# Keeping the partial sums of the seven-product pairs in two held PSUM banks

## The chip, the cores and the metric

The kernel runs on one core of one Trainium2 chip. The time is that of the device, in microseconds (us), from launch to end of one execution; the median of three runs of the kernel before is 1907.0 us (1905.99 to 1907.22).

## The reference

The reference is a trunk of two layers over 512 tokens of 1024 channels, in float32. Each layer has a feed-forward block, a token mixer (a convolution module in the first, stick-breaking attention in the second) and another feed-forward block. The change concerns the feed-forward blocks alone:

```
def swiglu_ffn(x, w_gate, w_up, w_down):
    return (jax.nn.silu(x @ w_gate) * (x @ w_up)) @ w_down
...
    h = h + HALF_STEP * swiglu_ffn(rms_norm(h, ffn1_norm[layer]), ...)
```

`w_gate` and `w_up` are 1024 x 2816 and `w_down` is 2816 x 1024, for each of the four blocks.

## The kernel before, in words

**Layout.** Channels lie on the 128 partitions, the 512 tokens along the free dimension, so the 1024 channels are eight tiles of 128 x 512, and the 2816 features of a block are 22 tiles, `f` = 0 to 21, worked in three thirds (`THIRDS`: 0 to 7, 8 to 15, 16 to 21). The four blocks are `ffn(0)` to `ffn(3)`. To keep float32 accuracy every operand is split into a rounded high part and a rest (`split`, L249 on ScalarE for the high part, L250 on VectorE for the rest), and every product is three matmuls: high by high, high by low, low by high.

**An ordinary pair.** For a feature tile, gate and up are two products of eight channel tiles and three matmuls each: 48 matmuls of 512 columns into two PSUM banks (L397 to L399). VectorE multiplies both banks by the norm's factor `rb` (L609, L611), ScalarE takes the Silu (L610), VectorE multiplies gate by up (L612), and the result is split into `hhi`, `hlo`. After a third, eight down products (`pd`) go to one bank each and are added to the residual stream by VectorE (L631).

**A seven-product pair.** In `ffn(1)` to `ffn(3)` the 32 tiles named in `SEVEN` (11, 10 and 11 of them) are made in another way, by the function `seven` (from L532): gate and up, the two halves of the channels and the two halves of the tokens form a 2 x 2 block product, which takes seven half-size products in place of eight:

```
SEVEN = {1: (5, 6, 8, 9, 11, 12, 14, 16, 17, 19, 20),
...
for q in range(NC // 2):
    PE.matmul(d, a[0], b[0], ...); PE.matmul(d, a[0], b[1], ...); PE.matmul(d, a[1], b[0], ...)
```

So a product is 12 matmuls of 256 columns (L555 to L557), and a pair 84. The products are named by their left operand: `11`, `12`, `22` (quarters of the weights) and `s1` to `s4` (sums of quarters, made on VectorE by `sevens`, L344 to L350). Their right operands are halves of `norm.x` (in the trace `xhi_f`, `xlo_f`) or sums `t` (`thi`, `tlo`). In the trace `11` and `12` are the matmuls with `xhi_f`/`xlo_f` and `whi`/`wlo`; `s1`, `s2` those with `sh`/`sl`; `s3`, `22` those with `thi`/`tlo` and `whi`/`wlo`; `s4` those with `uh`/`ul`.

The four results, gate (`tg`) and up (`tu`) for each half of the tokens, are these sums:

- gate, first half: `11` + `12`
- gate, second half: `11` + `s2` + `s1` + `s4`
- up, second half: `11` + `s2` + `s3` + `s1`
- up, first half: `11` + `s2` + `s3` + `22`

Before the change a pair takes three banks, `at_[0]` to `at_[2]`, of the seven of the pool `ps`. ScalarE copies `11` and `s1` to SBUF (`m1`, `m5`, L560 and L564); VectorE makes `v6` = `s2` + `m1` (L562) and `v7` = `s2` + `s3` + `m1` (L566), adds these to the banks (L568, L574, L575) and multiplies by `rb` (L571, L572, L576).

**Order.** Tiles, slots and semaphores come from the framework. The order in which each engine takes its instructions is fixed when the program is built: the text's order sets the priority, and an instruction whose operands would not be there is passed by later ones that can go. In the trace the matmuls of one pair stand among those of the next pair and of ordinary pairs. In the trace each engine then goes through its list in order: one that waits holds up those behind it. The next weights are fetched when a unit is taken (`unit`, `fetch`): DMA by the SyncE queue, then the split on ScalarE and VectorE, with three buffers of `raw`, `whi` and `wlo`, and for the second half of a seven-product pair's weights and for its sums one buffer each.

Of the kernel before, what the change touches and what calls it, by code (L numbers as in the profile page):

```python
# [6 lines left out]
F32 = mybir.dt.float32  # L7
# [7 lines left out]
P = 128  # L15
D = 1024
T = 512
# [181 lines left out]
def decoder_kernel(ctx, tc, xin, gu, dna, dnb, pw1, pw2, kq, wv, wo, out):  # L199
    nc = tc.nc  # L200
    V, A, G, PE = nc.vector, nc.scalar, nc.gpsimd, nc.tensor
# [35 lines left out]
    onesr = const.tile([P, P], F32R, name="onesr")  # L237
# [252 lines left out]
    def ffn(idx, norm, done, early=None, beside=None, sums=None, late=None, tail=None):  # L490
        with ExitStack() as c:
            hp = pool(c, f"hid{idx}")
            if beside is not None:
                pp_ = pool(c, f"beside{idx}")
            ps = pool(c, f"ps{idx}", space=PSUM)
            beside_hidden[0] = hp
            rb = norm.factor(ps) if idx else None
            halves = [slice(0, T // 2), slice(T // 2, T)]
            right = []

            def right_sums(q):


                x = []
                for k in (2 * q, 2 * q + 1):
                    f = tp.tile([P, T], F32, name=f"xs{idx}_{k}", tag="sq", bufs=2)
                    V.tensor_add(f, *(y.bitcast(F32) for y in norm.x[k]))
                    x.append(f)
                b11, b12, b21, b22 = (y[:, h] for y in x for h in halves)
                t = hp.tile([P, 2 * T], F32, name=f"ts{idx}_{q}", tag="st", bufs=STS)  # L510
                t1, t2, t3, t4 = (t[:, j * T // 2 : (j + 1) * T // 2] for j in range(4))
                V.tensor_sub(t1, b12, b11)
                V.tensor_sub(t2, b22, t1)
                V.tensor_sub(t3, b22, b12)
                V.tensor_sub(t4, b21, t2)
                tiles = [sums_at(q, o) for o in range(2)]
                for o, (h, l) in enumerate(tiles):
                    split(h, l, t[:, o * T : (o + 1) * T])
                right.append(tiles)
# [12 lines left out]
            def seven(n, tg, tu):  # L532
                w = unit()

                def x(row, h):
                    return lambda q: [y[:, halves[h]] for y in norm.x[2 * q + row]]

                def t(j):
                    return lambda q: [y[:, halves[j % 2]] for y in right[q][j // 2]]


                at_ = [
                    ps.tile([P, T], F32, name=f"pg{n}_{j}", tag="ps", bufs=7)[:, : T // 2]
                    for j in range(3)
                ]
                m1, m5, v6, v7 = (
                    hp.tile([P, T // 2], F32, name=f"{m}_{n}", tag=m, bufs=1)
                    for m in ("m1", "m5", "v6", "v7")
                )

                def product(j, left, rhs, first):
                    for q in range(NC // 2):
                        a, b, d = w[left](q), rhs(q), at_[j]
                        last_ = q == NC // 2 - 1
                        PE.matmul(d, a[0], b[0], start=first and q == 0, stop=False, skip_group_check=True)  # L555
                        PE.matmul(d, a[0], b[1], start=False, stop=False, skip_group_check=True)  # L556
                        PE.matmul(d, a[1], b[0], start=False, stop=last_, skip_group_check=True)  # L557

                product(0, "11", x(0, 0), True)
                A.copy(m1, at_[0])  # L560
                product(1, "s2", t(1), True)
                V.tensor_add(v6, at_[1], m1)  # L562
                product(2, "s1", t(0), True)
                A.copy(m5, at_[2])  # L564
                product(1, "s3", t(2), False)
                V.tensor_add(v7, at_[1], m1)  # L566
                product(2, "s4", x(1, 1), False)
                V.tensor_add(tg[:, halves[1]], at_[2], v6)  # L568
                product(0, "12", x(1, 0), False)
                product(1, "22", t(3), False)  # L570
                V.tensor_mul(tg[:, halves[1]], tg[:, halves[1]], rb[:, halves[1]])  # L571
                V.tensor_mul(tg[:, halves[0]], at_[0], rb[:, halves[0]])  # L572
                last[0] = A.activation(tg, tg, AF.Silu)
                V.tensor_add(tu[:, halves[1]], v7, m5)  # L574
                V.tensor_add(tu[:, halves[0]], at_[1], m1)  # L575
                V.tensor_mul(tu, tu, rb)  # L576

            for third, (f0, f1) in enumerate(THIRDS):
                hid = []
                for f in range(f0, f1):  # L580
                    n = f"{idx}_{f}"
                    if f in SEVEN.get(idx, ()):
                        tg = hp.tile([P, T], F32, name=f"tg{n}", tag="tg", bufs=2)
                        tu = hp.tile([P, T], F32, name=f"tu{n}", tag="tu", bufs=2)
                        seven(n, tg, tu)
                        V.tensor_mul(tu, tu, tg)  # L586
                        hi = hp.tile([P, T], F32R, name=f"hhi{n}", tag="hhi", bufs=8)
                        lo = hp.tile([P, T], F32R, name=f"hlo{n}", tag="hlo", bufs=8)
                        split(hi, lo, tu)
                        hid.append((hi, lo))  # L590
                        continue
                    pt = [ps.tile([P, T], F32, name=f"pg{n}_{o}", tag="ps", bufs=7) for o in range(2)]
                    if rb is None:
                        w = [unit() for o in range(2)]
                        for i, k in enumerate(norm.order):
                            for o in range(2):
                                mm3(pt[o], at(w[o], k * P, P), norm.x[k], i == 0, i == NC - 1)
                        with tc.issue_after(last[0].ins):
                            for k in range(NC):
                                norm.square(k)  # L600
                        rb = norm.factor(ps)
                    else:
                        for pp in pt:
                            w = unit()
                            for i, k in enumerate(norm.order):
                                mm3(pp, at(w, k * P, P), norm.x[k], i == 0, i == NC - 1)
                    tg = hp.tile([P, T], F32, name=f"tg{n}", tag="tg", bufs=2)
                    tu = hp.tile([P, T], F32, name=f"tu{n}", tag="tu", bufs=2)
                    V.tensor_mul(tg, pt[0], rb)  # L609
                    last[0] = A.activation(tg, tg, AF.Silu)  # L610
                    V.tensor_mul(tu, pt[1], rb)  # L611
                    V.tensor_mul(tu, tu, tg)  # L612
                    hi = hp.tile([P, T], F32R, name=f"hhi{n}", tag="hhi", bufs=8)
                    lo = hp.tile([P, T], F32R, name=f"hlo{n}", tag="hlo", bufs=8)
                    split(hi, lo, tu)
                    hid.append((hi, lo))
                    if f < NC // 2 and idx in SEVEN:
                        right_sums(f)
                    if early is not None and f == f0:
                        early(third, rb)  # L620
                    if beside is not None and (third or f > 1):
                        with tc.issue_after(last[0].ins):
                            beside(pp_)
                if third == 2 and late is not None:
                    late()
                for d in range(NC - TAIL if tail is not None and third == 2 else NC):
                    w = unit()
                    pd = ps.tile([P, T], F32, name=f"pd{idx}_{third}_{d}", tag="ps", bufs=7)
                    for j in range(f1 - f0):
                        mm3(pd, at(w, j * P, P), hid[j], j == 0, j == f1 - f0 - 1)  # L630
                    V.scalar_tensor_tensor(  # L631
                        res[d], pd, 0.5, res[d], op0=ALU.mult, op1=ALU.add
                    )
                    if third == 2:
                        done(d)
                    if beside is not None and d in (2, 5):
                        with tc.issue_after(last[0].ins):
                            beside(pp_)
# [5 lines left out]
    with ExitStack() as c:  # L644
        wm = pool(c, "wm")
        ps = pool(c, "pswm", space=PSUM)
# [7 lines left out]
    first = [opened() for o in range(2)]  # L654
# [51 lines left out]
    with ExitStack() as c:  # L706
        cv = pool(c, "cv")
        ps = pool(c, "pscv", space=PSUM)
        mshift = cv.tile([P, P], F32R, name="mshift")
        V.tensor_scalar_mul(mshift, ones, -1.0 / P)  # L710
        rb = tp.tile([P, T], F32, name="r_mix_0", tag="r", bufs=1)
# [327 lines left out]
        for d in SECOND[3:]:  # L1039
            w = None if d in HELD else unit()  # L1040
# [14 lines left out]
    with ExitStack() as c1:  # L1055
# [30 lines left out]
        with ExitStack() as c:  # L1086
            ap = pool(c, "at")
            ps = pool(c, "psat", space=PSUM)
# [391 lines left out]
```

## Time and profile before

| | |
|---|---|
| median of three runs | 1907.0 us |
| span of the profiled execution, first to last instruction | 1904.9 us |
| TensorE (PE) busy | 1884.1 us |
| VectorE (DVE) busy | 1318.5 us |
| ScalarE (ACT) busy | 872.7 us |
| matmuls | 10236 |

The profiled execution has no time of its own beside its span; the span is 2.1 us under the median of the runs. In the rows of the profile, times are in us unless marked ns; PE is the matmul, PEld the weight load that runs beside it. A row of the grouped lines gives line, engine, operation, output and inputs, shape, count, then busy time in us, mean ns of one, and after the second bar the engine's idle time just before them with what ended it. A row of the timeline gives start, duration, engine, line, operation and tiles. In the windows view a row has the stretch, its length, and the busy time and instruction count of each engine.

### The profile page before, as it was taken

What the parts mean: (1) busy time and instruction counts of PE and PEld (TensorE: products, weight loads), DVE (VectorE), ACT (ScalarE), POOL (GpSimd) and SP (SyncE); (2) the same over time, 40 slices, a digit from 0 to 9 for tenths busy, and PEclk for the clock granted to TensorE, in tenths of its full rate; (3) what the DMA queues carried; (4) which work ended last, traced back from release to release, by engine and by line L of the source; (5) the groups of instructions that cost most, each with busy time, mean ns of one, the idle gap of its engine ahead of it and who ended that gap; (6) DMA issues with size and microseconds to landing.
All of it is one profiled execution on the core that took longest, in us unless ns stands there. A gap on an engine that the chain in (4) does not pass through costs nothing.

```text
span 1904.9 us, 26577 instructions
## 1 busy us (share of the span) xinstructions
PE 1884.1 (99%) x10236; PEld 1630.4 (86%) x10236; DVE 1318.5 (69%) x2139; ACT 872.7 (46%) x1385; POOL 288.1 (15%) x267
## 2 busy tenths in 40 slices
PE   9999999999999999999999999999999999999997
PEld 7888888878998889898888988888888788898896
DVE  6544434589869577576775857778989688676575
ACT  5423424586644234244333423446778644343333
POOL 0212302079700000000000000004554100000001
PEclk9999999999999999999999999999999999999998
DMA  5756746444422323333433232442323133332322
GB/s 203 251 180 232 275 146 216 158 172 144 161 78 89 105 89 117 100 94 96 143 111 100 89 111 89 127 155 83 89 70 93 49 123 100 100 95 95 111 86 70
DMA packets 74254, 237.84 MB, mean 125 GB/s; under 512 B 8464, under 2 KB 11152, under 8 KB 74128
## 3 DMA queue, kind: packets, MB, share of 16 engines
q1 hardware_dynamic: 65776, 209.41, 34.0%
q10 hardware_dynamic: 8352, 26.74, 3.8%
q8 instruction: 80, 1.31, 0.3%
q14 instruction: 46, 0.38, 0.1%
HBM read 200.46 MB, written 31.46 MB: 122 GB/s over the span
## 4 chain that ended last, share of the span: by engine, by line
PE 94%; DVE 2%; POOL 1%; ACT 1%; issue 1%; DMA 0%; POOLq 0%; DVEq 0%; ACTq 0%
PE pg L397 11%; PE pg L398 11%; PE pg L399 11%; PE pd L398 8%; PE pd L397 8%; PE pd L399 8%; PE pg L557 6%; PE pg L556 6%; PE pg L555 6%; PE z L1192 2%; PE pa L397 1%; PE pa L398 1%; PE pa L399 1%; PE pv L397 1%; PE pk L397 1%
## 5 line engine op out<-in xcount | busy, mean ns | idle before, releaser
L249 ACT CAST whi<-raw 128x1024 fp32r<-128x1024 f32 (+2 forms) x310 | 313.2, 1013 | 634.6 <-PE pd L398 226.8
L250 DVE TENSOR_TENSOR wlo<-raw,whi 128x1024 fp32r<-128x1024 f32 (+2 forms) x310 | 367.8, 1191 | 43.1 <-ACT whi L249 42.7
L398 PE MATMUL pg<-xlo_f,whi 128*128 128x512 f32 x896 | 349.7, 391 | 0.0
L397 PE MATMUL pg<-xhi_f,whi 128*128 128x512 f32 x896 | 349.0, 391 | 0.6 <-ACT whi L249 0.6
L399 PE MATMUL pg<-xhi_f,wlo 128*128 128x512 f32 x896 | 349.4, 390 | 0.0
L398 PE MATMUL pd<-hlo,whi 128*128 128x512 f32 x686 | 266.2, 389 | 0.0
L399 PE MATMUL pd<-hhi,wlo 128*128 128x512 f32 x686 | 265.1, 389 | 0.0
L397 PE MATMUL pd<-hhi,whi 128*128 128x512 f32 x686 | 264.1, 389 | 0.0
L397 PEld LDWEIGHTS pg<-xhi_f,whi 128*128 128x128 f32 x896 | 169.0, 189 | 35.2 <-ACT whi L249 1.5
L399 PEld LDWEIGHTS pg<-xhi_f,wlo 128*128 128x128 f32 x896 | 168.6, 188 | 34.7 <-DVE wlo L250 0.3
L398 PEld LDWEIGHTS pg<-xlo_f,whi 128*128 128x128 f32 x896 | 168.8, 188 | 33.6
L631 DVE SCALAR_TENSOR_TENSOR xpar<-pd,xpar 128x512 f32<-128x512 f32 x93 | 63.7, 689 | 170.6 <-PE pd L399 170.6
L399 PEld LDWEIGHTS pd<-hhi,wlo 128*128 128x128 f32 x686 | 128.8, 188 | 26.8
L397 PEld LDWEIGHTS pd<-hhi,whi 128*128 128x128 f32 x686 | 128.8, 188 | 26.7
L398 PEld LDWEIGHTS pd<-hlo,whi 128*128 128x128 f32 x686 | 128.8, 188 | 26.6
L1092 POOL TENSOR_SCALAR_AFFINE_SELECT tri<-ones 128x128 f32<-128x128 f32 x1 | 0.6, 592 | 703.7 <-DVE tu L612 703.7
L250 POOL TENSOR_TENSOR plo<-praw,phi 128x1024 fp32r<-128x1024 f32 x24 | 59.0, 2461 | 275.7 <-ACT phi L249 273.9
L875 POOL TENSOR_TENSOR ws<-ws,pr 128x256 f32<-128x256 f32 (+1 forms) x90 | 91.0, 1023 | 58.2 <-ACT pr L873 54.6
L249 ACT CAST hhi<-tu 128x512 fp32r<-128x512 f32 x88 | 54.3, 621 | 87.9 <-DVE tu L586 49.2
L886 DVE SCALAR_TENSOR_TENSOR pc<-gl,xpar,pc 128x512 f32<-128x512 f32 (+1 forms) x145 | 88.3, 646 | 3.9 <-PE pc L865 2.2
L611 DVE TENSOR_TENSOR tu<-pg,r_f 128x512 f32<-128x512 f32 x56 | 38.6, 689 | 74.2 <-PE pg L399 74.2
L556 PE MATMUL pg<-tlo,whi 128*128 128x256 f32 x256 | 72.5, 283 | 0.0
(359 smaller groups left out, 4195.0 us busy)
## 6 DMA issues: line engine op xcount, KB each, us to landing
raw<-in_gu_dram SPq DMA_DIRECT2D x174, 512.0 KB, 3.5
raw<-in_dna_dram SPq DMA_DIRECT2D x64, 512.0 KB, 3.6
praw<-in_pw_dram SPq DMA_DIRECT2D x24, 512.0 KB, 4.4
aparth<-phi ACTq DMA_DIRECT2D x24, 512.0 KB, 2.7
apartl<-plo ACTq DMA_DIRECT2D x24, 512.0 KB, 3.8
raw<-in_dnb_dram SPq DMA_DIRECT2D x32, 384.0 KB, 3.4
whi<-aparth SPq DMA_DIRECT2D x21, 512.0 KB, 3.3
wlo<-apartl SPq DMA_DIRECT2D x21, 512.0 KB, 4.2
```

The lines of the kernel that those rows point to most:

```text
L249: ins = A.copy(dst_hi, src)
L250: (G if on_pool else V).tensor_sub(dst_lo, src, dst_hi.bitcast(F32))
L397: PE.matmul(ps, w[0], x[0], start=first, stop=False)
L398: PE.matmul(ps, w[0], x[1], start=False, stop=False)
L399: PE.matmul(ps, w[1], x[0], start=False, stop=last)
L555: PE.matmul(d, a[0], b[0], start=first and q == 0, stop=False, skip_group_check=True)
L556: PE.matmul(d, a[0], b[1], start=False, stop=False, skip_group_check=True)
L557: PE.matmul(d, a[1], b[0], start=False, stop=last_, skip_group_check=True)
L611: V.tensor_mul(tu, pt[1], rb)
L631: V.scalar_tensor_tensor(res[d], pd, 0.5, res[d], op0=ALU.mult, op1=ALU.add)
L875: add("G", 1.28 * f + 0.1 * half, lambda pr=pr: G.tensor_add(accp, accp, pr()[:, at0]), r=[pr], w=[at_], rank=rank)
L886: add("V", 0.66 * f + 0.06 * half, lambda x=x, q=q: V.scalar_tensor_tensor(pc(), x(), q, pc(), op0=ALU.mult, op1=ALU.add), r=[gl], w=[pc], ...
```

## The change

A pair takes two banks of its own, `g0` and `m`, and two banks `u0`, `g1` are held from the first feature tile of the block to the last seven-product pair, shared by all its pairs. ScalarE copies `11` from `g0` into `u0`, on which `s2` accumulates; it copies that sum from `u0` into `g1`, on which `s4` accumulates, while `s3` and then `22` accumulate on `u0`. `v6`, `v7` and `m1` go; `m5` gets two buffers. Two matmuls at the first feature tile of each of the three blocks write `u0` and `g1` once (`seed_banks`), so that later ones add to what stands there. The products, their number, and the tiles of `SEVEN` stay; the order of the products in the text changes from `11`, `s2`, `s1`, `s3`, `s4`, `12`, `22` to `11`, `s1`, `s2`, `12`, `s3`, `s4`, `22`.

```
-                at_ = [ps.tile([P, T], F32, name=f"pg{n}_{j}", tag="ps", bufs=7)[:, : T // 2] for j in range(3)]
-                m1, m5, v6, v7 = (hp.tile([P, T // 2], F32, name=f"{m}_{n}", tag=m, bufs=1) for m in ("m1", "m5", "v6", "v7"))
+                g0, m = (ps.tile([P, T], F32, name=f"pg{n}_{j}", tag="ps", bufs=7)[:, : T // 2] for j in range(2))
+                u0, g1 = seeds
+                m5 = hp.tile([P, T // 2], F32, name=f"m5_{n}", tag="m5", bufs=2)
...
-                product(0, "11", x(0, 0), True)
-                A.copy(m1, at_[0])
-                product(1, "s2", t(1), True)
-                V.tensor_add(v6, at_[1], m1)
-                product(2, "s1", t(0), True)
-                A.copy(m5, at_[2])
-                product(1, "s3", t(2), False)
-                V.tensor_add(v7, at_[1], m1)
-                product(2, "s4", x(1, 1), False)
-                V.tensor_add(tg[:, halves[1]], at_[2], v6)
-                product(0, "12", x(1, 0), False)
-                product(1, "22", t(3), False)
+                product(g0, "11", x(0, 0), True)
+                A.copy(u0, g0)
+                product(m, "s1", t(0), True)
+                A.copy(m5, m)
+                product(u0, "s2", t(1), False)
+                A.copy(g1, u0)
+                product(g0, "12", x(1, 0), False)
+                V.tensor_mul(tg[:, halves[0]], g0, rb[:, halves[0]])
+                product(u0, "s3", t(2), False)
+                V.tensor_add(tu[:, halves[1]], u0, m5)
+                product(g1, "s4", x(1, 1), False)
+                V.tensor_add(tg[:, halves[1]], g1, m5)
                 V.tensor_mul(tg[:, halves[1]], tg[:, halves[1]], rb[:, halves[1]])
-                V.tensor_mul(tg[:, halves[0]], at_[0], rb[:, halves[0]])
                 last[0] = A.activation(tg, tg, AF.Silu)
-                V.tensor_add(tu[:, halves[1]], v7, m5)
-                V.tensor_add(tu[:, halves[0]], at_[1], m1)
-                V.tensor_mul(tu, tu, rb)
+                product(u0, "22", t(3), False)
+                V.tensor_mul(tu[:, halves[1]], tu[:, halves[1]], rb[:, halves[1]])
+                V.tensor_mul(tu[:, halves[0]], u0, rb[:, halves[0]])
+
+            seeds = []
+
+            def seed_banks():
+                for j in range(2):
+                    d = ps.tile([P, T], F32, name=f"seed{idx}_{j}", tag="ps", bufs=7)[:, : T // 2]
+                    PE.matmul(d, onesr, norm.x[0][0][:, : T // 2], start=True, stop=True)
+                    seeds.append(d)
...
                     if f < NC // 2 and idx in SEVEN:
+                        if not f:
+                            seed_banks()
                         right_sums(f)
```

More of the change, by code (lines that the diff above doesn't have):

```diff
@@ L539, in t, with product @@
                     return lambda q: [y[:, halves[j % 2]] for y in right[q][j // 2]]
-                at_ = [
+                g0, m = (
                     ps.tile([P, T], F32, name=f"pg{n}_{j}", tag="ps", bufs=7)[:, : T // 2]
[L544 to L548, printed above, removed]
-                )
-                def product(j, left, rhs, first):
+                    for j in range(2)
+                )
+                u0, g1 = seeds
+                m5 = hp.tile([P, T // 2], F32, name=f"m5_{n}", tag="m5", bufs=2)
+                def product(d, left, rhs, first):
                     for q in range(NC // 2):
-                        a, b, d = w[left](q), rhs(q), at_[j]
+                        a, b = w[left](q), rhs(q)
                         last_ = q == NC // 2 - 1
```

## The prediction

> **What bounds the kernel now.** I read the page's first two parts, then the stages of the three blocks with seven-product pairs, then who waits on PE, then the groups by shape, then the timeline of two pairs that follow each other.
>
> ```profile
> span 1904.9 us, 26577 instructions
> PE 1884.1 (99%) x10236; PEld 1630.4 (86%) x10236; DVE 1318.5 (69%) x2139; ACT 872.7 (46%) x1385; POOL 288.1 (15%) x267
> PEclk9999999999999999999999999999999999999998
> ```
>
> PE is busy for all but 20.8 us of the span, at the full granted clock but for the last slice. Where those 20.8 us lie decides what the change can win. The windows from the first to the last matmul of `ffn(1)`, `ffn(2)` and `ffn(3)`, and one of three feature tiles (two pairs and an ordinary one), whose columns after start and length are PE, PEld, DVE and ACT:
>
> ```profile
> 558.00:912.00 354.00, 354.00 (x2000) 311.85 (x2000) 247.10 (x381) 133.53 (x181) 0.00 (x0) 1.00 0.32 99
> 910.00:1258.00 348.00, 348.00 (x1934) 305.21 (x1933) 247.25 (x381) 135.56 (x183) 3.03 (x7) 1.00 0.36 115
> 1542.00:1875.00 333.00, 333.00 (x1908) 294.48 (x1907) 230.68 (x360) 123.53 (x166) 0.00 (x0) 1.00 0.30 96
> 683.80:715.00 31.20, 31.20 (x218) 29.26 (x217) 22.92 (x35) 13.49 (x19) 0.00 (x0) 1.00 0.28 84
> ```
>
> In all three blocks PE is busy from end to end. The list of PE's waits in the whole run has sixteen rows; its head and its only row of a gate or up product are
>
> ```profile
> PE pb_out1v L1351 <- ACT dg_out L1342: 4.9, 1, 4.9
> ...
> PE pg L397 <- ACT whi L249: 0.6, 1, 0.6
> ```
>
> and that one lies outside the three blocks, where PE has no gap. No matmul of a pair (L555 to L557) stands in it. So the blocks are bound by the number of matmuls times PE's step, and the idle 20.8 us belong to the start, the convolution, the attention and the end, which the change leaves alone.
>
> **The change part by part.** First the groups that it touches or queues behind:
>
> ```profile
> L555 PE MATMUL pg<-thi,sh 128*128 128x256 f32 x256 | 71.7, 283 | 0.0
> L250 DVE TENSOR_TENSOR wlo<-raw,whi 128x1024 fp32r<-128x1024 f32 x266 | 329.3, 1241 | 42.5 <-ACT whi L249 42.1
> L249 ACT CAST whi<-raw 128x1024 fp32r<-128x1024 f32 x266 | 279.6, 1052 | 569.2 <-PE pd L398 198.7 <-PE pg L398 181.8 <-PE pg L556 69.5
> L398 PEld LDWEIGHTS pg<-xlo_f,whi 128*128 128x128 f32 x896 | 168.8, 188 | 33.6
> L631 DVE SCALAR_TENSOR_TENSOR xpar<-pd,xpar 128x512 f32<-128x512 f32 x93 | 63.7, 689 | 170.6 <-PE pd L399 170.6
> L576 DVE TENSOR_TENSOR tu<-tu,r_f 128x512 f32<-128x512 f32 x32 | 22.1, 690 | 0.8
> L566 DVE TENSOR_TENSOR v<-pg,m 128x256 f32<-128x256 f32 x32 | 13.5, 423 | 25.8 <-PE pg L557 25.7
> L575 DVE TENSOR_TENSOR tu<-pg,m 128x256 f32<-128x256 f32 x32 | 13.5, 423 | 40.0 <-PE pg L557 40.0
> L571 DVE TENSOR_TENSOR tg<-tg,r_f 128x256 f32<-128x256 f32 x32 | 13.5, 422 | 0.7
> L562 DVE TENSOR_TENSOR v<-pg,m 128x256 f32<-128x256 f32 x32 | 13.4, 420 | 7.5 <-PE pg L557 7.5
> L560 ACT COPY m<-pg 128x256 f32<-128x256 f32 x32 | 11.8, 370 | 21.2 <-PE pg L557 20.9
> ```
>
> *VectorE.* `v6` and `v7` (420 and 423 ns) and one of the later adds (L575, 423) go; one multiplication of 512 columns (690) becomes two of 256 (422 each, by L571). That is 0.420 + 0.423 + 0.423 + 0.690 - 2 x 0.422 = 1.11 us less for each of 32 pairs, 35.6 us in all. It lies beside PE, which waits for none of it: 0 on the path.
>
> *ScalarE.* Two copies become three. The trace has no copy from PSUM to PSUM; the nearest row is the copy from PSUM to SBUF, 370 ns. I take that; from below it cannot be under zero, from above I allow a doubling, 0.74. The third copy adds 11.8 us to an engine that works 13.49 of 31.20 us where pairs follow each other: 0 on the path by itself.
>
> *TensorE.* The 84 matmuls of a pair stay, in other order. Six new ones write the held banks. They are of 256 columns, and such matmuls start 0.12 us after each other (timeline below): 6 x 0.12 = 0.7 us on the path. Bounds: 0, if they fall into a gap, to 6 x 0.283 = 1.7.
>
> *The handovers.* Here the change adds waits, all on `u0`. The timeline of tiles 8 and 9 of `ffn(1)`:
>
> ```profile
> 685.11 0.28 PE L557 MATMUL pg<-xhi_f,wlo 128*128 128x256 f32 x1
> 685.23 0.28 PE L555 MATMUL pg<-thi,sh 128*128 128x256 f32 x1
> 685.43 0.37 ACT L560 COPY m<-pg 128x256 f32<-128x256 f32 x1 [0.56 <-PE pg L557]
> ...
> 686.94 0.42 DVE L562 TENSOR_TENSOR v<-pg,m 128x256 f32<-128x256 f32 x1 [0.82 <-PE pg L557]
> ...
> 688.11 0.28 PE L555 MATMUL pg<-xhi_f,whi 128*128 128x256 f32 x1
> ...
> 689.55 0.28 PE L555 MATMUL pg<-thi,whi 128*128 128x256 f32 x1
> ...
> 693.75 0.28 PE L557 MATMUL pg<-xhi_f,wlo 128*128 128x256 f32 x1
> ...
> 696.39 0.28 PE L557 MATMUL pg<-thi,wlo 128*128 128x256 f32 x1
> ...
> 696.59 1.05 ACT L249 CAST whi<-raw 128x1024 fp32r<-128x1024 f32 x1 [1.45 <-PE pg L556]
> ...
> 696.71 0.42 DVE L575 TENSOR_TENSOR tu<-pg,m 128x256 f32<-128x256 f32 x1 [1.63 <-PE pg L557]
> ...
> 697.54 0.36 ACT L560 COPY m<-pg 128x256 f32<-128x256 f32 x1
> ```
>
> The first product's last matmul ends at 685.11 + 0.28 = 685.39 and ScalarE starts at 685.43: 0.04 us from product to reader (the same at 696.39 + 0.28 and 696.71 for `22` and VectorE). A product of twelve takes 12 x 0.12 = 1.44 us (688.11 to 689.55 is one). In the text's order each handover has one product as cover, of which 0.28 - 0.12 = 0.16 go on the tail of the product before:
>
> - `11` to `s2`: `s1` covers 1.44. Needed: 0.16 + 0.04 + 0.37 = 0.57. Spare 0.87, or 0.50 with a copy of 0.74.
> - `s2` to `s3`: the copy to `g1`, covered by `12`. The same, spare 0.87.
> - `s3` to `22`: an addition of 0.42 in place of the copy, covered by `s4`. Spare 0.82.
> - `22` to the next pair's `s2`, where pairs follow each other (14 of the 31 steps, by `SEVEN`): 0.16 + 0.04 + 0.42 + 0.04 + 0.37 = 1.03 against the next `11` and `s1`, 2.88. Spare 1.85. In the trace the next pair's `s2` starts before this pair's `22`, so PE must take its matmuls in another order; `s1`, `12` and those of the ordinary pair stand for it.
>
> What eats the spare time is what the reader's engine is at. Behind a weight cast just begun (1.05) the copy comes 1.05 - 0.87 = 0.18 late, twice in a pair; behind a weight rest (1.24) the addition comes 1.24 - 0.82 = 0.42 late. If all three met the worst in each pair and PE had nothing else, that would be (0.18 + 0.18 + 0.42) x 32 = 25 us. The other end is 0, or below zero only if PE had waits to lose, and it has none. I take 0: ScalarE is idle for more than half of that window, VectorE loses 1.11 us a pair, 2.2 of the 22.92 of that window, and PE is given matmuls of other products where one is late. That the present order leaves room is seen in the same rows: the copy ended at 685.80 and the product that writes its bank again, `12`, started at 688.11, 2.3 us later; `v6` ended at 687.36 and `s3` started at 689.55, 2.2 us later. Behind the waiting copies stand weight casts on ScalarE, which VectorE's rests and then PE need; their idle row says that they wait for PE (569 us), so they have room.
>
> *Sum.* 1904.9 + 0.7 + 0 = 1905.6 for a profiled execution. The median of the runs lies 2.1 above the span, which I carry over: 1907.7.
>
> **The rivals.**
>
> *A, the copies hold PE up (slower).* Place: ScalarE's queue in front of `s2` and `s3`. For it: the second pair's `11` ends at 693.75 + 0.28 = 694.03, but its copy starts at 697.54, 3.51 us later, because the cast at 696.59, which waits for PE, stands in front. Before, nothing but a late product needed that copy; after, `s2` does. It decides where the queue delays a reader by over 0.82 to 0.87 us and PE has no other matmul ready. Price: up to the 25 us worked out above, 1932.7; a third of it, 8.3, gives 1916.0. Against: the 14 steps between neighbours have 1.85 spare, and what PE needs next was ready about 2 us early.
>
> *B, a gain after all (faster).* VectorE's 35.6 us could only count where PE waits for VectorE, and no such row exists in the blocks. What remains is PE's step: 1% of 84 x 32 x 0.12 = 323 us would be 3.2 us, so a gain of 2%, 6.4 us, would give 1901.3. The row of weight loads shows 33.6 us of idle over 896, 0.04 each, with no releaser: it is part of the step, not a wait. The Trainium skill ("Trainium Kernel Development and Optimization", opening part on reading a trace) judges the distance to the roof by how busy weight loading is and not by matmul rows; by it the 86% of PEld would leave room for a gain. The three windows do show PEld under PE, 311.85 against 354.00, but it is the same 0.04 us in each step, which no bank or copy changes.
>
> *C, banks run short (slower).* Two of seven banks are held, so ordinary pairs and down products have five. If each of the 8 x 3 x 3 = 72 down products of the blocks waited for its reader, 0.04 + 0.69 (L631) each, that is 53 us: 1960. Against: that reader itself idles 170.6 us waiting for PE, so a bank is free shortly after its product ends. The Trainium skill ("PSUM — Partial Sum Buffer", summary of rules) advises prompt evacuation because the space is tight, and speaks so against held banks; the trace shows no wait of PE for a bank here.
>
> **How the numbers follow.** The forecast, PE still without a gap in the three blocks, has 0.73; A 0.20; B 0.05; C 0.02. A difference of under 0.2%, 3.8 us, is about what cannot be told from no change. The forecast lies within it, with 0 to 1.7 us for the new matmuls and 1.1 us of spread between the runs shown. So: faster 0.05, same 0.73, slower 0.22. The range goes from 1904.5 (the lowest run less 1.5) to 1916.0, A at a third of its price; above it stay about 0.13 of A and C, below it 0.04.
>
> **What would show it.** Right: PE busy over the whole of the three blocks, no row of a pair's matmul among PE's waits, six more matmuls, VectorE some 36 us less busy, ScalarE some 12 more. Wrong by A: PE rows that wait for ScalarE's copies into `u0` or `g1`, or for the addition on `u0`. Wrong by C: PE rows of `pd` or `pg` that wait for their banks' readers. Wrong in size: copies into PSUM far from 0.37 us, or a step of 256 columns other than 0.12.

## The result, and the profile after

The changed kernel takes 1989.7 us (median of four runs, 1989.4 to 1990.6) against 1907.1 for the kernel before: 1.0434 times as long, 95% interval 1.0419 to 1.0449. The forecast was no difference, in a range from 1904.5 to 1916.0. The time lies far above the range, and above what either slower rival could have cost (A 1932.7, C 1960).

The page of the kernel after, its span and the busy times:

```profile
span 1987.3 us, 26609 instructions
PE 1916.6 (96%) x10242; PEld 1639.9 (83%) x10242; DVE 1281.4 (64%) x2075; ACT 1006.4 (51%) x1511; POOL 280.1 (14%) x267
```

Six matmuls more, as they should be, and VectorE 37.1 us less busy. But ScalarE is 133.7 us busier where a third copy should have brought 11.8, with 126 instructions more where 32 are the new copies. Most of that lies in the attention, between `ffn(2)` and `ffn(3)`, in which no line was changed: ScalarE works 122.7 us more there, and PE has gaps. The stretch from the first projection matmul to the first matmul of `ffn(3)`, by the windows view of the kernel before and of the kernel after (start and end, length, then PE, PEld, DVE, ACT and POOL, the granted clock, and the share and GB/s of the DMA):

```profile
1259.30:1537.30 278.00, 273.17 (x1506) 230.15 (x1507) 234.45 (x405) 186.90 (x348) 98.09 (x92) 1.00 0.29 85
```

```profile
1261.60:1618.70 357.10, 303.87 (x1507) 239.94 (x1506) 230.86 (x407) 309.62 (x443) 91.27 (x92) 0.96 0.22 67
```

The attention takes 79.1 us more of the 82.4 by which the span grew. The three blocks, which the change did touch, in the same view of the kernel after, in the order `ffn(2)`, `ffn(1)`, `ffn(3)`:

```profile
906.50:1261.60 355.10, 353.97 (x1957) 309.61 (x1958) 239.35 (x364) 141.05 (x197) 3.03 (x7) 1.00 0.36 114
552.30:906.50 354.20, 353.05 (x1994) 310.42 (x1993) 236.44 (x362) 138.50 (x194) 0.00 (x0) 1.00 0.31 99
1618.70:1968.20 349.50, 349.23 (x2011) 309.02 (x2010) 228.03 (x351) 132.36 (x185) 0.00 (x0) 1.00 0.29 92
```

The same stretches, from the first matmul of a block to that of what follows, in the kernel before:

```profile
905.40:1259.30 353.90, 353.03 (x1955) 309.06 (x1954) 251.26 (x388) 138.78 (x188) 3.03 (x7) 1.00 0.36 117
553.30:905.40 352.10, 352.10 (x1993) 310.27 (x1992) 247.24 (x382) 133.56 (x182) 0.00 (x0) 1.00 0.31 98
1537.30:1885.80 348.50, 348.50 (x2009) 308.77 (x2009) 239.16 (x373) 128.64 (x174) 0.00 (x0) 1.00 0.29 93
```

The blocks grew by 2.1 (`ffn(1)`), 1.2 (`ffn(2)`) and 1.0 (`ffn(3)`): 4.3 us together. What stands ahead of them, where the text is the same, was 1.0 us shorter in this execution, and what follows them as long as before. 79.1 + 4.3 - 1.0 = 82.4.

What fills ScalarE in the attention is seen in the groups by line of the kernel after. The group does not exist in the kernel before:

```profile
L1210 ACT ACT_TABLE_LOAD x46 | 59.0, 1283 | 0.8
L1241 ACT ACT_TABLE_LOAD x26 | 33.4, 1283 | 0.5
L1209 ACT ACT_TABLE_LOAD x21 | 26.9, 1283 | 0.4
```

These are loads of activation tables (ACT_TABLE_LOAD in the trace). They stand ahead of the two Exp (L1209, L1241) and the Ln (L1210) of the attention: 93 x 1.283 = 119.3 us. The attention of the kernel before has not one. The timeline of ScalarE at its head, in the kernel after, shows how they come:

```profile
1295.72 1.28 ACT L1209 ACT_TABLE_LOAD   x1
1297.02 0.63 ACT L1209 ACTIVATE a<-a 128x512 f32<-128x512 f32 x1
...
1298.57 1.28 ACT L1210 ACT_TABLE_LOAD   x1
1299.86 0.63 ACT L1210 ACTIVATE a<-a 128x512 f32<-128x512 f32 x1
1300.51 1.28 ACT L1209 ACT_TABLE_LOAD   x1
```

Exp and Ln take turns, and at each turn a table is loaded. Both kernels contain one line that is there to prevent this: at the head of the attention (L1254 before, L1262 after) a table set that holds both functions, `natural_log_exp_and_others`, is loaded once, and `issue_after(last[0].ins)` places it behind the last Silu of `ffn(2)`, where `last[0]` is the last Silu in the order of the text, that of tile 21. The attention's own instructions are in turn placed behind the load. The two timelines of ScalarE around it, kernel before and kernel after:

```profile
1219.81 0.62 ACT L573 ACTIVATE tg<-tg 128x512 f32<-128x512 f32 x1
1220.33 0.62 ACT L610 ACTIVATE tg<-tg 128x512 f32<-128x512 f32 x1
1220.97 1.28 ACT L1254 ACT_TABLE_LOAD   x1
```

```profile
1223.20 0.63 ACT L616 ACTIVATE tg<-tg 128x512 f32<-128x512 f32 x1
1223.84 1.28 ACT L1262 ACT_TABLE_LOAD   x1
1225.14 0.62 ACT L249 CAST kvh<-kvb 128x512 fp32r<-128x512 f32 x1
1225.78 1.28 ACT L570 ACT_TABLE_LOAD   x1
1227.65 0.64 ACT L570 ACTIVATE tg<-tg 128x512 f32<-128x512 f32 x1 [0.59 <-DVE tg L569]
```

Before, the Silu of tile 20, a seven-product pair (L573), came 0.5 us ahead of the Silu of tile 21 (L610), and the load behind both. After, tile 21 (L616) has overtaken tile 20 (L570). The load stands behind tile 21 alone, the Silu of tile 20, whose sum is late, comes 2.5 us after it has ended and brings its own table back (1225.78), and the set for the attention is gone before the attention begins. From there each Exp and each Ln is given a table of its own.

### The profile page after: what moved, and what is told of

It is laid out like the page before. It is cut to its first block, busy times and chain, and to the rows that moved or that the text cites. A ratio compares the mean times of both kernels' runs of the same rounds, so it can differ in the third digit from the quotient of the medians.

```text
span 1987.3 us, 26609 instructions
## 1 busy us (share of the span) xinstructions
PE 1916.6 (96%) x10242; PEld 1639.9 (83%) x10242; DVE 1281.4 (64%) x2075; ACT 1006.4 (51%) x1511; POOL 280.1 (14%) x267
## 4 chain that ended last, share of the span: by engine, by line
PE 82%; ACT 11%; issue 3%; DVE 2%; POOL 1%; DMA 1%; POOLq 0%; ACTq 0%; DVEq 0%
PE pg L397 10%; PE pg L399 10%; PE pg L398 10%; PE pd L398 8%; PE pd L397 8%; PE pd L399 8%; PE seed L553 3%; PE seed L554 3%; PE seed L555 3%; PE pg L553 2%; PE pg L554 2%; PE pg L555 2%; ACT L1210 2%; ACT L1241 1%; PE pa L397 1%
## 5 line engine op out<-in xcount | busy, mean ns | idle before, releaser
L617 DVE TENSOR_TENSOR tu<-pg,r_f 128x512 f32<-128x512 f32 x56 | 38.5, 688 | 72.8 <-PE pg L399 72.6
L1211 DVE SCALAR_TENSOR_TENSOR a<-z,a 128x512 f32<-128x512 f32 (+1 forms) x48 | 31.0, 647 | 65.6 <-ACT a L1210 58.8
```

## The experiments

**Theory and rivals.** Theory: the whole loss in the attention comes from the order of two Silus and one table load, and the order turned because `s4`, on whose sum the Silu of a pair waits, now stands behind two copies in a row (the experiments bear out the first half; the second is left open below). Rivals: the third copy or the held banks load ScalarE so that it lags in the attention; the new order of the products, or any sharing of a bank, turns the order of the Silus. Each ratio below is to the kernel before as it ran on the same chip, with its 95% interval.

**The load behind both Silus.** The changed kernel, which now keeps its Silus in a list, `silus`, in the order of the text, and places the load behind the last two of them:

```
-            with tc.issue_after(last[0].ins):
+            with tc.issue_after(silus[-1].ins), tc.issue_after(silus[-2].ins):
                 table = A.preload_act_table_set("natural_log_exp_and_others")
```

> The changed kernel, with one thing more: the table load for the attention is placed behind the Silu of tile 20 as well as behind that of tile 21 of the third feed-forward block. Theory (table order): five table loads in the run instead of 99, the attention stretch back from 357 to about 278 us, the Silu of tile 20 before the load; total 1989.7 - 79.1 = 1910.6, of which 4.4 us over the kernel before stay in the three blocks. Rival (the third copy, or held banks, load ScalarE so that it holds the attention up): total stays at 1980 or more.

Measured: 1912.3 us, 1.0026 (1.0016 to 1.0036), where before had 1907.3. The timeline of ScalarE has the two Silus still in the turned order (L618 is tile 21, L571 tile 20), but both ahead of the load, and the window of the attention is as before the change:

```profile
1224.56 0.63 ACT L618 ACTIVATE tg<-tg 128x512 f32<-128x512 f32 x1
1228.05 0.63 ACT L571 ACTIVATE tg<-tg 128x512 f32<-128x512 f32 x1 [2.35 <-DVE tg L570]
1228.70 1.28 ACT L1265 ACT_TABLE_LOAD   x1
```

```profile
1262.20:1540.80 278.60, 274.12 (x1508) 230.93 (x1507) 235.92 (x407) 187.90 (x350) 97.83 (x92) 0.99 0.29 86
```

All that the change does to banks, copies and VectorE is in this kernel, and the attention takes 278.6 us. 77.4 of the 82.6 us (1989.7 less 1907.1) are gone; 5.0 stay over the 1907.3 of before, where the expectation put 4.4 to the blocks; the time came 1.7 above the expected 1910.6.

**The same fault without the change.** The kernel before, with the load behind the Silu of tile 19 (`silus[-3]`), so that two Silus follow it.

> The kernel before, without any part of the change; only the table load for the attention is placed behind the Silu of tile 19 instead of that of tile 21, so that two Silus come after it. Theory (table order): some 95 more table loads in the attention, whose stretch goes from 278 to about 357 us; total 1907.1 + 79 = 1986 (1980 to 1992). Rival: one table load too many costs 1.3 us on an engine that is half idle, and the total stays at 1907 to 1909.

Measured: 1985.9 us, 1.0413 (1.0399 to 1.0428). The groups by line, and the window of the attention:

```profile
L1205 ACT ACT_TABLE_LOAD x46 | 59.0, 1283 | 0.8
L1236 ACT ACT_TABLE_LOAD x26 | 33.4, 1283 | 0.5
L1204 ACT ACT_TABLE_LOAD x21 | 26.9, 1283 | 0.4
```

```profile
1258.60:1615.90 357.30, 304.85 (x1507) 240.34 (x1508) 231.21 (x405) 308.68 (x442) 90.84 (x92) 0.96 0.22 66
```

The same 93 loads and the same 357 us, with nothing of the change in the kernel. Both sides are shown: with the load behind both Silus the loss is absent, though all of the change is there and the two Silus still stand in the turned order; with Silus behind the load the loss is there, without the change.

**The order of the products alone.** The kernel before, its three banks and `v6`, `v7`, with the products in the changed order.

```
-                product(1, "s2", t(1), True)
-                V.tensor_add(v6, at_[1], m1)
                 product(2, "s1", t(0), True)
                 A.copy(m5, at_[2])
+                product(1, "s2", t(1), True)
+                V.tensor_add(v6, at_[1], m1)
+                product(0, "12", x(1, 0), False)
+                V.tensor_mul(tg[:, halves[0]], at_[0], rb[:, halves[0]])
                 product(1, "s3", t(2), False)
...
```

> The kernel before with its three banks per pair and v6, v7, but with the products in the order of the changed kernel, and the table load where it was. Theory (what delays the Silu of tile 20 is the shared bank u0, not the order of the text): five table loads, attention 278 us, total 1907.1 within 2 us. Rival (the order alone delays it): 99 loads and about 1986.

Measured: 1906.1 us, 0.9995 (0.9986 to 1.0004). No table load in the attention, and tile 20's Silu comes 2.1 us ahead of tile 21's (1217.24 and 1219.35), so the order of the products in the text alone does not turn the Silus.

**`s4` back on the bank of `s1`.** The changed kernel with its table load untouched; `u0` is still shared, but the sum on it is copied to SBUF and `s4` waits for no second copy.

```
-                u0, g1 = seeds
+                u0, = seeds
...
-                A.copy(g1, u0)
+                A.copy(v6, u0)
...
-                product(g1, "s4", x(1, 1), False)
-                V.tensor_add(tg[:, halves[1]], g1, m5)
+                product(m, "s4", x(1, 1), False)
+                V.tensor_add(tg[:, halves[1]], m, v6)
```

> The changed kernel with its table load where the change left it, but with u0 alone as held bank: the sum s2 on it is copied to SBUF (v6) and not to g1, and s4 accumulates on the bank of s1, as before the change; gate, second half, is that bank plus v6. Theory (s4 waits for two copies in a row, and so the Silu of tile 20 falls behind that of tile 21 and behind the table load): five table loads, attention 278 us, total 1907.3 + 0.4 (three seeds) + up to 3 for the waits of s2 on u0 = 1908 to 1911. Rival (any sharing of a bank by neighbouring pairs is enough to delay it): 99 table loads and about 1987.

Measured: 1911.2 us, 1.0023 (1.0014 to 1.0031), 0.2 us above the theory's 1908 to 1911. ScalarE's timeline:

```profile
1223.55 0.63 ACT L571 ACTIVATE tg<-tg 128x512 f32<-128x512 f32 x1
1224.08 0.62 ACT L617 ACTIVATE tg<-tg 128x512 f32<-128x512 f32 x1
1224.72 1.28 ACT L1263 ACT_TABLE_LOAD   x1
```

Tile 20 (L571) is ahead of tile 21 (L617) again, by the same 0.5 us as before the change, and the loss in the attention is gone although the load's line is the one that failed. So the shared `u0` alone does not turn the order; something that came with `g1` does. This kernel leaves out three things at once: the second copy ahead of `s4`, a second bank shared by neighbours, and a second held bank. Nor is it a copy that holds `s4` up in the run. In the kernel after, tile 20's copy into `g1` and the first matmul of its `s4` are

```profile
1217.88 0.36 ACT L562 COPY seed<-seed 128x256 f32<-128x256 f32 x1
1223.30 0.28 PE L553 MATMUL seed<-xhi_f,uh 128*128 128x256 f32 x1
```

The copy ended at 1218.24, 5 us before; in between PE took `12`, twelve matmuls of tile 21 and `s3`. In the whole trace of the kernel after no instruction waits for a copy into `g1`. The order is the one that was fixed when the program was built, and the trace does not show by which term of the build it turned.

**Two sets of held banks, used by turns.** As the first experiment, with four held banks, so that neighbouring pairs share none.

```
-                u0, g1 = seeds
+                u0, g1 = seeds[:2]
+                seeds[:] = seeds[2:] + seeds[:2]
...
-                for j in range(2):
+                for j in range(4):
```

> As the kernel with the table load behind both Silus, but with two sets of held banks that the pairs use by turns: four of seven banks held, twelve seeding matmuls instead of six. Theory (the handover of u0 between neighbouring pairs is what costs in the blocks, six times 0.4 us): those gaps go, 0.7 us of seeds come, total 1910.6 - 2.4 + 0.7 = 1909. Rival (three free banks are too few): PE waits for the readers of ordinary and down products, total above 1915.

Measured: 1922.5 us, 1.0081 (1.0068 to 1.0095). The gaps of 0.4 us ahead of `s2` on a held bank are gone, as the theory had it, but the rival outweighs that. The head of PE's waits, one stretch of the timeline at the start of `ffn(1)`, and the window of what follows the gap:

```profile
PE pg L397 <- DVE tg L618: 10.4, 3, 3.5
```

```profile
574.25 0.50 PE L397 MATMUL pg<-xhi_f,whi 128*128 128x512 f32 x1 [3.33 <-DVE tg L618]
...
575.97 0.63 PE L397 MATMUL pg<-xhi_f,whi 128*128 128x512 f32 x1
576.40 0.63 PE L398 MATMUL pg<-xlo_f,whi 128*128 128x512 f32 x1
```

```profile
575.30:578.90 3.60, 3.60 (x10) 2.81 (x9) 3.60 (x8) 1.76 (x3) 0.00 (x0) 0.53 0.09 35
```

With three free banks PE waits for the reader of the first ordinary pair, once in each block, 10.4 us in all: at the start of a block VectorE also makes the sums `t` and its queue is long (from 571.00 to 574.50 it is never idle). In `ffn(1)` the granted clock after that gap is 0.53 for some 3.6 us, and a matmul of 512 columns starts 0.43 us after the last in place of 0.227.

This kernel also bears on what turns the order. The Silus of tile 20 (L572) and tile 21 (L619) are here

```profile
1228.97 0.63 ACT L572 ACTIVATE tg<-tg 128x512 f32<-128x512 f32 x1
1229.60 0.63 ACT L619 ACTIVATE tg<-tg 128x512 f32<-128x512 f32 x1
```

Two copies in a row stand ahead of `s4`, and more banks are held than in the changed kernel, yet tile 20 is first; in the first experiment, which differs from this one in the sets of banks alone, it is second. So the two copies alone do not turn the order, nor does the number of held banks alone. What is left is that neighbouring pairs share `g1` as well as `u0`. No run tries that by itself, and any edit can shift the order that the build makes, so this part of the cause stays open.

**More pairs.** If the relief of VectorE is to be worth something, it is by more seven-product pairs. 38 tiles in place of 32, the table load behind the last three Silus, in three kernels:

```
-SEVEN = {1: (5, 6, 8, 9, 11, 12, 14, 16, 17, 19, 20), 2: (6, 8, 10, 11, 13, 14, 16, 17, 19, 20), ...
+SEVEN = {1: (5, 6, 7, 8, 9, 10, 12, 13, 14, 16, 17, 18, 20), 2: (5, 6, 8, 9, 10, 12, 13, 14, 16, 17, 18, 20), ...
```

> The changed kernel with the table load behind the last three Silus, and with 38 tiles made by seven products in place of 32, three in a row at most. Each saves 48 x 0.2267 - 84 x 0.12 = 0.8 us of matmuls, 4.8 in all. Theory (in the blocks it is now the handovers that cost, 0.4 us where two pairs follow each other): 1912.3 - 4.8 + about 10 more neighbours x 0.4 = 1911.5. Rival (VectorE's relief of 1.1 us a pair is what lets more pairs in): 1907.5.

> The kernel before, with the table load behind the last three Silus and the same 38 tiles made by seven products. If VectorE's work per pair, which the change cuts by 1.1 us, is what limits the number of pairs, PE waits for weights here and the time is at or above the 1907.3 of the kernel before; if it does not limit it, 1907.3 - 4.8 = 1902.5.

> The kernel with u0 alone held and s4 on the bank of s1, the table load behind the last three Silus, and the same 38 tiles. If the second copy's chain is what makes the handovers late: 1909.5 - 4.8 = 1904.7, under the kernel before. If the wait on u0 itself is: as the changed kernel with 38 pairs, some 1911.

Measured: the changed kernel 1935.4 us, 1.0145 (1.0129 to 1.016); the kernel before 1918.0, 1.0058 (1.0045 to 1.007); `s4` on the bank of `s1` 1943.1, 1.0191 (1.0177 to 1.0205). All are slower than with 32 pairs. Both expectations for the changed kernel missed, and both for the last; the one for the kernel before met the time of its first branch, but not its reason. PE's waits in the changed kernel and in the kernel before, each with 38 pairs:

```profile
PE seed L554 <- ACT seed L559: 11.8, 9, 1.3
...
PE seed L554 <- ACT seed L563: 3.7, 1, 3.7
```

```profile
PE pg L556 <- ACT m L565: 6.0, 6, 1.4
```

In the changed kernel `s2` waits for the copy into `u0` nine times, up to 1.3 us, and once 3.7 for the copy into `g1`; in the kernel before it is ScalarE's copy of `s1` that is late. In both, most of what PE waits for in the blocks is in ScalarE's queue; VectorE stands for 1.5 us of it in the kernel before with 38 pairs. The waits listed do not add up to the whole loss, and why weights come late in the last of the three (11.5 us of PE waiting for the cast of `whi`) stays open. No kernel tried here is faster than the kernel before by more than the noise.

## Why the prediction was wrong, point by point

**The step that failed** is the end of the part on what bounds the kernel: that the idle 20.8 us belong to "the start, the convolution, the attention and the end, which the change leaves alone". It leaves their text alone, not the state that ScalarE brings to them. The attention depends on an order between the last Silus of `ffn(2)` and one table load, and the change moved a Silu across it; in place of "alone" the runs showed 93 table loads and 79.1 us. That cost is no wait in the blocks, so none of the terms and rivals, all priced inside the blocks, could hold it. The part ahead of the prediction told that an engine's list is made from priorities and readiness; the prediction used that to argue that PE would find other matmuls, and did not ask what else is reordered with them. The trace of before would have shown the danger: three rows, 1219.81, 1220.33 and 1220.97, with 0.5 us between the two Silus, and a tile 20 whose chain the change made longer. It would not have shown that the order turns.

**VectorE** lost 37.1 us for the 35.6 worked out, with no effect on the path: right.

**ScalarE**: the copies into PSUM took what the row of the copy into SBUF gave. In the groups by line of the kernel after, the copy into `u0` and the one into `g1` are

```profile
L558 ACT COPY seed<-pg 128x256 f32<-128x256 f32 x32 | 11.7, 364 | 9.1 <-PE pg L555 9.1
L562 ACT COPY seed<-seed 128x256 f32<-128x256 f32 x32 | 11.6, 362 | 19.6 <-PE seed L555 19.6
```

so the term 11.8 was 11.6. Of the other 122.1 of ScalarE's 133.7, 120.6 us are 94 more loads of 1.283: the 93 of the attention and the one that tile 20's Silu brought. "0 on the path by itself" held for the copies as work.

**Handovers.** Taken as 0; they were 2.4 us. Rival A was at work, in its place and at a tenth of its price. The timeline of the kernel after between tiles 11 and 12 of `ffn(1)`:

```profile
717.14 0.28 PE L555 MATMUL seed<-thi,wlo 128*128 128x256 f32 x1
...
717.38 1.05 ACT L249 CAST whi<-raw 128x1024 fp32r<-128x1024 f32 x1 [0.35 <-PE seed L554]
717.46 0.43 DVE L573 TENSOR_TENSOR tu<-seed,r_f 128x256 f32<-128x256 f32 x1 [1.10 <-PE seed L555]
...
718.34 0.37 ACT L558 COPY seed<-pg 128x256 f32<-128x256 f32 x1
718.34 0.28 PE L555 MATMUL pg<-xhi_f,wlo 128*128 128x256 f32 x1
...
718.75 0.39 PE L553 MATMUL seed<-thi,sh 128*128 128x256 f32 x1
```

`22` of tile 11 ends at 717.42, VectorE reads it until 717.89, but the copy for tile 12 stands behind a weight cast until 718.34, and `s2` starts at 718.75. PE has matmuls of `11` for the pair after tile 12 up to 718.34 + 0.12, so 0.29 us are lost, and 0.10 at the next step. The spare time of 1.85 that the prediction gave this step was not there: tile 12's `11` and `s1` had run before `22` of tile 11 and could not cover it, and ten matmuls, 1.2 us, were what covered it in their place. Six of the 14 steps between neighbours look so, 6 x 0.4 = 2.4 us, and all six wait for the copy into `u0`. One wait for the cast of `sh` adds 1.1 (tile 11 of `ffn(2)`) and the six seeding matmuls 0.7. A wait of 0.9 us for a weight cast is new at the end of `ffn(1)`, and one as long at the end of `ffn(2)` is gone, so these two cancel. That is 4.2 of the 4.3 us by which the blocks grew, and most of the 5.0 us that the first experiment leaves. With the table in its place the time, 1912.3, lies inside the range; whether it would have been "the same" (under 0.2%) is not decided by 0.26% with an interval from 0.16 to 0.36.

**Banks and gain.** In the three blocks no PE row of the kernel after waits for a bank's reader, so rival C stayed out with five banks; with three it came, at the start of the blocks, which the prediction had not named. There was no gain, as rival B's low chance had it. Two figures of the prediction are off, without effect on its sum: the steps between pairs that share banks are 29, not 31 (32 pairs in three blocks), and what weight loads leave idle in the three windows is 0.02 us a step (42 of 354.00 us over 2000 matmuls in the first), not 0.04.

## What to carry to other kernels

An activation table is state that an engine carries from stage to stage, and a load that is placed behind "the last" use in the text guards nothing once the build may reorder uses: tie it to every use that could come late. Before a change that lengthens a chain is priced inside its own stage, look at what stands within a microsecond of the chain's end on each engine, at stage ends above all. And when an engine gains instructions that the diff does not contain, as here 94 table loads, count those first: the groups of operations that exist in one profile and not in the other named the cause at once.

## What the runs showed of the hardware

A table load takes 1.283 us, and the next activation starts 0.02 us after it (1295.72 + 1.28 and 1297.02). The Trainium skill ("ScalarE: Activation LUTs", "What ACT_TABLE_LOAD costs") gives the same 1283 ns for the load and a drain of 1380 beside it; in the rows above there is no such pause, so a switch costs 1.3 us here and not 2.7. 93 loads, 119.3 us of ScalarE, made a stretch 79.1 us longer in which ScalarE had been 67% busy (186.90 of 278.00) and became 87% busy.

After PE idled 3.33 us in `ffn(1)` of the kernel with two sets, the granted clock fell to about half for some 3.6 us, about 1 us after PE had begun again. The Trainium skill ("TensorE: Matmul & The Clock Gate", "Part 1: The HAM clock gate") tells of a window of about 3.4 us without work after which the clock is halved; the step of 0.43 us in place of 0.227 agrees with a halved clock, and the gap is about as long as that window. The gaps in the two later blocks of that kernel were 3.53 us each, and the clock fell after only one of them: it was 1.00 from 932.20 to 937.00, behind the gap in `ffn(2)`, and 0.52 from 1568.80 to 1572.30, behind the gap in `ffn(3)`. So of two gaps of the same length one cost the clock and the other did not.
